# Early up-projection products in other PSUM banks, activation splits in another pool, kept norm chunks through DRAM: a two-layer encoder trunk on one Trainium2 core

## The chip, the cores and the metric

One core of one Trainium2 chip runs the whole program. The metric is device microseconds of one execution; 2956.74 us is the median of three runs of the kernel before (2948.64 to 2969.05).

The engines are TensorE (PE, matmuls into PSUM banks), VectorE (DVE), ScalarE (ACT), GpSimd (POOL), and SyncE (SP), which issues the DMAs. Each engine takes its instructions in a fixed order and waits at the head of it.

## What is computed

A trunk of two layers on x of 1024 tokens by 1024 features, all in fp32. Each layer mixes tokens by four head groups (pooling, chunked band attention, sparse attention, latent attention), projects them back, and then has a gated feed-forward part:

```python
    x = x + gt1 * (mix @ w_out[l])
    h = rmsnorm(x, g_ffn[l]) * (1.0 + sc2) + sh2
    f = (jax.nn.silu(h @ ffn_w1[l]) * (h @ ffn_w3[l])) @ ffn_w2[l]
    x = x + gt2 * f
return rmsnorm(x, g_final)
```

The feed-forward width is 2816, which is 22 blocks of 128 (NF = 22). `sc2`, `sh2` and `gt2` come from `c_act @ w_mod`, one vector for all tokens.

## The kernel before

**Numbers.** An fp32 product is made of three matmuls of a faster type: each operand is split in a high part, cast by ACT (L154 for weights to `wh`, L1102 to `ws`), and a low part, the difference, by POOL or DVE (L162, `wl`). A matmul below is one of 128x128 weights with 512 tokens. The activations stand transposed: features on partitions, tokens along the row, in two halves of 512 tokens.

**Up projection.** Pairs of blocks for both token halves are made by Strassen's scheme with seven products instead of eight (`product`, L1136), from sums of weights (`su`, `ws`) and sums of the normalised activations. `combos` (L1106) makes the activation sums u1 to u4 on DVE, from a chunk tile t0 of the first half and one t1 of the second. Some products need only the first token half: `up_pre` (L1167) makes those early, directly from w1 and w3 of a block, with its matmuls on L1181: 24 matmuls for one of the two weights, and their halves are copied to `xx`.

**Norm and what stands around it.** `norm2(g, r)` normalises token half g before the feed-forward part. It begins with the statistics: squares (ACT L359, DVE L360), their sum over features by matmuls with ones (L329), a reciprocal root on DVE, a broadcast by four L346 matmuls (two instructions each in the trace's count), and ACT's copy of it to R (L348). Then for k = 0 to 3 two chunks are made (L388, L394, L396, L399, L403) to a tile `t` of 512 KB and to the split `h`. For the first half `t` is kept to serve as t0 later. Between `norm2(0)` and `norm2(1)` stand the output projection of the second half (`proj_c(1)`, matmuls L184 to L186, the addition to x on DVE, L1090) and the early products. `norm2(1)` calls `combos` for each k.

**Down pass.** For each token half the 22 blocks f are summed over eight PSUM banks (L1331): `load(f)` gets a row of `ffn_w2` (DMA to `raw`, `wh` by ACT, `wl` by POOL), `act(f, g)` gets the activation from DRAM (`su`, then a split `ws`). x comes back from DRAM first (L1335). In the second half the first four f are kept (LATE = 4) until the eighth bank is free. Between the halves of layer 0 the statistics and the first norm of layer 1 run.

**Memory and order.** `slabs` is a pool of 34 tiles of 4 KB per partition, which x, h, t, `wh` and `wl` of the down pass share. A second pool in this part of the program has a ring of nine tiles `w` (`wslab`), two `su`, and there are two `raw` buffers. PSUM has eight banks under four names: mm 2, s 2, tr 3, pv 1. The output projection uses mm. The Tile scheduler simulates a timeline and so decides the order in each engine's queue; priorities (`high_priority`) and free buffers steer it. One queue, SP's, issues nearly all DMAs, in order: weights, spills, and the loads of `w_mod` whose sums (L271 to L274) are made for layer 1 during layer 0's feed-forward part.

`bank(i)` gives the bank of a product by its number:

```python
tag, bufs = (("mm", 2), ("s", 2), ("tr", 3), ("tr", 3), ("mm", 2), ("s", 2), ("tr", 3), ("pv", 1))[i]
```

Of the kernel before, what the change touches and what calls it, by code (L numbers as in the profile page):

```python
# [8 lines left out]
F32 = mybir.dt.float32  # L9
F32R = mybir.dt.float32r  # L10
# [8 lines left out]
DEPTH = 2  # L19
# [32 lines left out]
LATE = 4  # L52
LAST = 2
ALL7 = (1, 6, 5, 7, 2, 3, 4)
PRE = 2
# [14 lines left out]
class Trunk:  # L70
# [144 lines left out]
    def late_consts(self):  # L215
# [18 lines left out]
        if DEPTH > 1:  # L234
            self.xspill = self.dram.tile([KD, 128, S], F32, name="xspill")
        self.x2spill = [self.dram.tile([KD, 128, S], F32, name=f"x2spill{l}") for l in range(DEPTH)]
        self.aspill = [self.dram.tile([NF, 128, S], F32, name=f"aspill{l}") for l in range(DEPTH)]
        self.pspill = [self.dram.tile([2, 128, S], F32, name=f"pspill{l}") for l in range(DEPTH)]
# [859 lines left out]

    def split_tile(self, src, eng):

        w = self.wslab("ws")
        self.nc.scalar.activation(w[:, 0:512], src, AF.Copy)  # L1102
        self.sub_lo(w[:, 512:1024], src, w[:, 0:512], eng)
        return w

    def combos(self, t0, t1, b, db, c, out):  # L1106
# [3 lines left out]
        nc = self.nc  # L1110
# [12 lines left out]
        v.scalar_tensor_tensor(out=u2, in0=t1[:, 1, :], scalar=be, in1=u1, op0=ALU.add, op1=ALU.subtract)  # L1123
        split(2, u2, nc.vector)
        v.scalar_tensor_tensor(out=u3, in0=t1[:, 1, :], scalar=db[:, c:c + 1], in1=t1[:, 0, :],
                               op0=ALU.add, op1=ALU.subtract)
        split(3, u3, nc.gpsimd)
        v.scalar_tensor_tensor(out=u4, in0=t0[:, 1, :], scalar=be, in1=u2, op0=ALU.add, op1=ALU.subtract)
        split(4, u4, nc.vector)

# [37 lines left out]
    def up_pre(self, l, fa, H):  # L1168


        nc = self.nc
        xx = self.slab("xx", F32, (128, 2, 512))
        V = self.slab("v", F32, (128, 512))
        for i, name in enumerate(("w1", "w3")):
            wh, wl = self.load_w(self.a[name][l, fa])
            p = self.bank(i)
            for o, B in ((0, H[0][0:4]), (512, H[0][4:8])):
# [104 lines left out]
    def ffn(self, l, x, H, T, side, between):  # L1282
# [34 lines left out]
        def act(f, g):  # L1317
            t = self.rp.tile([128, 1024], F32, tag="su", bufs=NSUM, name=self.nm("su"))[:, 0:512]
            nc.sync.dma_start(out=t, in_=self.aspill[l][f][:, HALVES[g]])
            with self.tc.high_priority(offset=PRIO):  # L1320
                return self.split_tile(t, nc.vector)

# [52 lines left out]
    def mixer(self, l, x, H, spill, side, between, feed=None, first=None):  # L1375
# [193 lines left out]

        kept = []  # L1570
        HT = {}

        def norm2(g, r):
# [7 lines left out]
            for k in range(4):  # L1581
# [4 lines left out]
                if g == 0:  # L1586
                    kept.append(t)
                else:
                    self.combos(kept[k], t, b, db, k, HT)
                    kept[k] = None  # L1590
            for d in range(KD):
# [274 lines left out]
```

## Time and profile before

| | us |
|---|---|
| median of three runs (lowest, highest) | 2956.74 (2948.64, 2969.05) |
| profiled execution | 2957.3 |
| its span, from the first to the last instruction | 2955.4 |
| granted TensorE clock in it, mean | 0.935 |
| PE busy in the span | 2697.8 (91%) |
| VectorE, ScalarE, GpSimd busy | 1857.7, 1316.2, 1146.3 |
| moved by DMA | 305.92 MB |

Times in the trace count from the start of the span. Layer 0's first norm2 lies at 740 to 776 us, its up projection runs to 1268, its down pass to about 1554; layer 1's norm2 begins near 2188. A granted clock of 1.00 is 2.4 GHz, of 0.50 it is 1.2 GHz, and a value between is a mean over both. A bracket behind an instruction gives the engine's idle time just before it and what ended it. An engine that is idle off the critical path costs nothing.

### The profile page before, as it was taken

The numbers are of one execution on the slowest core, as the hardware profiler recorded it, in microseconds if no ns is written. First come the engines' busy times: TensorE is split into PE (matmuls) and PEld (weight loads), VectorE is DVE, ScalarE is ACT, GpSimd is POOL, SyncE is SP. The second block draws the span as 40 slices with busy tenths as digits, with TensorE's granted clock in tenths as the row PEclk, the third lists the DMA queues.
The fourth block names the chain that finished last, engine by engine and source line by source line (L and its number), as shares of the span: only waits on it lengthen the run. The fifth ranks groups of instructions, "written<-read, shape, count | busy, mean of one in ns | idle before, by whom it ended". The sixth has DMA issues, their size and how long they took to land.

```text
span 2955.4 us, 35110 instructions
## 1 busy us (share of the span) xinstructions
PE 2697.8 (91%) x12304; PEld 2144.3 (73%) x12304; DVE 1857.7 (63%) x3610; ACT 1316.2 (45%) x2536; POOL 1146.3 (39%) x672
## 2 busy tenths in 40 slices
PE   4897988899779999998899889998977999999998
PEld 3776757778547888887688667787765788888876
DVE  7579867775687566543335898788476743334452
ACT  4454767854423333332324547776443333333330
POOL 4242134441445555452623320113234655555630
PEclk9898979999769999999899989799988999999998
DMA  6102133233232344462431021112222222226540
GB/s 244 53 19 86 60 127 96 76 129 104 100 125 93 124 158 166 166 217 82 144 138 53 11 92 54 56 40 65 101 79 79 97 82 86 86 75 227 175 149 29
DMA packets 109873, 305.92 MB, mean 104 GB/s; under 512 B 13312, under 2 KB 14208, under 8 KB 109696
## 3 DMA queue, kind: packets, MB, share of 16 engines
q1 hardware_dynamic: 109696, 303.68, 30.1%
q8 instruction: 96, 1.57, 0.2%
q14 instruction: 81, 0.66, 0.1%
HBM read 245.11 MB, written 51.18 MB: 100 GB/s over the span
## 4 chain that ended last, share of the span: by engine, by line
PE 53%; DVE 10%; ACT 2%; DMA 2%; issue 2%; POOL 1%; SPq 0%; DVEq 0%; ACTq 0%; POOLq 0%
PE tr L1136 11%; PE mm L1136 7%; PE tr L1331 5%; PE s L1136 4%; PE pv L1136 3%; PE s L1331 3%; PE mm L1331 3%; DVE jv L544 2%; DMA raw<-ffn_w 2%; PE pv L1331 2%; PE mm L184 2%; PE mm L186 2%; PE mm L185 1%; PE tr L679 1%; DVE t L394 1%
## 5 line engine op out<-in xcount | busy, mean ns | idle before, releaser
L162 POOL TENSOR_TENSOR wl<-raw,wh 128x1024 fp32r<-128x1024 f32 (+1 forms) x158 | 375.6, 2381 | 629.0 <-ACT wh L154 349.6
L1136 PE MATMUL tr<-h,ws 128*128 128x512 f32 x1512 | 385.3, 403 | 20.3 <-POOL h L162 8.1
L1136 PEld LDWEIGHTS tr<-h,ws 128*128 128x128 f32 x1512 | 286.1, 190 | 105.0 <-POOL h L162 13.5
L162 POOL TENSOR_TENSOR ws<-su,ws 128x512 fp32r<-128x512 f32 x176 | 262.8, 1499 | 244.3 <-ACT ws L1102 220.7
L1102 ACT ACTIVATE ws<-su 128x512 fp32r<-128x512 f32 x264 | 163.3, 627 | 374.8 <-PE tr L1136 72.7
L162 DVE TENSOR_TENSOR ws<-su,ws 128x512 fp32r<-128x512 f32 x88 | 150.3, 1716 | 264.9 <-ACT ws L1102 264.7
L154 ACT ACTIVATE wh<-raw 128x1024 fp32r<-128x1024 f32 (+1 forms) x138 | 141.3, 1027 | 278.8 <-DMA raw<-ffn_w 182.9
L1136 PE MATMUL mm<-h,ws 128*128 128x512 f32 x912 | 237.6, 404 | 14.1 <-ACT ws L1102 8.9
L1136 PEld LDWEIGHTS mm<-h,ws 128*128 128x128 f32 x912 | 173.6, 192 | 61.7 <-ACT ws L1102 13.6
L162 POOL TENSOR_TENSOR ws<-raw,ws 128x512 fp32r<-128x512 f32 x108 | 157.1, 1458 | 127.9 <-ACT ws L1102 112.3
L541 ACT ACTIVATE ja<-score,tk_t 128x384 bf16<-128x384 f32 (+2 forms) x160 | 146.0, 913 | 121.8 <-DVE tk_t L563 86.1
L655 ACT ACTIVATE P<-P,mx 128x128 f32<-128x128 f32 (+1 forms) x192 | 142.9, 745 | 76.1 <-DVE mx L652 60.6
L1331 PE MATMUL tr<-ws,wh 128*128 128x512 f32 x528 | 167.6, 399 | 0.0
L682 ACT ACTIVATE Th<-tr 128x512 fp32r<-128x512 f32 (+3 forms) x288 | 127.8, 467 | 83.1 <-PE tr L679 75.2
L162 DVE TENSOR_TENSOR Tl<-tr,Th 128x512 fp32r<-128x512 f32 (+2 forms) x232 | 131.7, 587 | 32.3 <-ACT Th L682 31.4
L679 PE MATMUL tr<-ident,P 128*128 128x128 f32 x816 | 142.2, 290 | 7.1 <-DVE y L712 5.8
L1136 PE MATMUL s<-h,ws 128*128 128x512 f32 x528 | 141.9, 412 | 2.8 <-DVE yy L1224 2.8
L1102 ACT ACTIVATE ws<-raw 128x512 fp32r<-128x512 f32 x108 | 68.0, 629 | 169.7 <-PE tr L1136 105.7
L1331 PE MATMUL mm<-ws,wh 128*128 128x512 f32 x352 | 112.3, 399 | 14.0 <-ACT wh L154 14.0
L679 PEld LDWEIGHTS tr<-ident,P 128*128 128x128 f32 x816 | 107.2, 153 | 24.4 <-DVE y L712 7.4
L1136 PEld LDWEIGHTS s<-h,ws 128*128 128x128 f32 x528 | 103.0, 197 | 29.0 <-DVE yy L1224 3.2
L544 DVE TENSOR_SCALAR_CACHE_REDUCE jv<-up,tk_t 128x896 bf16<-128x896 bf16 (+3 forms) x128 | 120.8, 944 | 4.5 <-POOL up L522 1.9
(415 smaller groups left out, 6889.9 us busy)
## 6 DMA issues: line engine op xcount, KB each, us to landing
raw<-w SPq DMA_DIRECT2D x100, 512.0 KB, 3.5
raw<-ffn_w SPq DMA_DIRECT2D x88, 512.0 KB, 3.5
mraw<-w_mod SPq DMA_DIRECT2D x48, 512.0 KB, 6.0
t<-w_mod SPq DMA_DIRECT2D x96, 256.0 KB, 4.6
su<-aspill SPq DMA_DIRECT2D x88, 256.0 KB, 3.0
aspill<-act SPq DMA_DIRECT2D x32, 512.0 KB, 3.3
raw<-w_fm SPq DMA_DIRECT2D x30, 512.0 KB, 3.9
x2spill<-x SPq DMA_DIRECT2D x32, 256.0 KB, 2.2
```

The source lines that it names most:

```text
L154: self.nc.scalar.activation(out, in_, AF.Copy)
L162: (eng or self.nc.vector).tensor_tensor(out=out, in0=in_, in1=hi.bitcast(F32), op=ALU.subtract)
L184: self.nc.tensor.matmul(out, lh, rh, start=(i == 0), stop=False)
L186: self.nc.tensor.matmul(out, ll, rh, start=False, stop=(stop and i == n - 1))
L541: nc.scalar.activation(ja, score[t], AF.Sign, bias=c, scale=-1.0, accum_out=o)
L544: v.tensor_scalar(out=jv, in0=up[t] if step < 16 else score[t], scalar1=c, scalar2=0.0, op0=ALU.is_ge, op1=ALU.subtract, accum_out=o)
L655: nc.scalar.activation(P[:, 0:nk], P[:, 0:nk], AF.Exp, bias=m[:, j:j + 1], scale=-1.0, accum_out=st["rs"][:, i:i + 1])
L679: nc.tensor.transpose(p[:, i * 128:(i + 1) * 128], P[:, (kts[n] - k0) * 128:(kts[n] - k0 + 1) * 128], self.ident)
L682: nc.scalar.activation(Th[:, cs].bitcast(F32) if len(js) <= few else Th[:, cs], p[:, cs], AF.Copy)
L1102: self.nc.scalar.activation(w[:, 0:512], src, AF.Copy)
L1136: self.nc.tensor.matmul(p, u, r, start=first and k == 0 and i == 0, stop=k == 3 and i == 2, skip_group_check=not first)
L1331: nc.tensor.matmul(p, u, r, start=(f == 0 and i == 0), stop=(f == NF - 1 and i == 2))
```

## The change

There are three edits that move work; a fourth gives a name, `LOENG`, to the engine of two splits and leaves it as it is (`nc.vector`).

- A: `up_pre` takes bank 1 and 2 for the products of w1 and w3 (names s and tr) instead of 0 and 1 (mm and s).
- B: in the down pass `act` asks `split_tile` for a tile of `slabs` for the activation's split `ws` instead of one of the nine of the ring `w`.
- C: the four chunk tiles `t` of `norm2(0)` are stored to DRAM (`tspill`, 512 KB each) and loaded again as `t0` in `norm2(1)`, instead of being kept in four slabs between. Per layer these are four stores and four loads more.

```diff
+LOENG = lambda nc: nc.vector
...
+        self.tspill = [self.dram.tile([4, 128, 2, 512], F32, name=f"tspill{l}") for l in range(DEPTH)]
...
-    def split_tile(self, src, eng):
-
-        w = self.wslab("ws")
+    def split_tile(self, src, eng, base=False):
+
+        w = self.slab("ws", F32R) if base else self.wslab("ws")
         self.nc.scalar.activation(w[:, 0:512], src, AF.Copy)
         self.sub_lo(w[:, 512:1024], src, w[:, 0:512], eng)
         return w
...
-        split(2, u2, nc.vector)
+        split(2, u2, LOENG(nc))
...
-        split(4, u4, nc.vector)
+        split(4, u4, LOENG(nc))
...
         for i, name in enumerate(("w1", "w3")):
             wh, wl = self.load_w(self.a[name][l, fa])
-            p = self.bank(i)
+            p = self.bank(1 + i)
...
-                return self.split_tile(t, nc.vector)
+                return self.split_tile(t, nc.vector, True)
...
-        kept = []
         HT = {}
...
                 if g == 0:
-                    kept.append(t)
+                    nc.sync.dma_start(out=self.tspill[l][k], in_=t)
                 else:
-                    self.combos(kept[k], t, b, db, k, HT)
-                    kept[k] = None
+                    t0 = self.slab("t0", F32, (128, 2, 512))
+                    nc.sync.dma_start(out=t0, in_=self.tspill[l][k])
+                    self.combos(t0, t, b, db, k, HT)
```

The new lines move every line number behind them by one or two: L1181 is L1183 in the changed kernel, L329 is L331, L346 is L348, L154 is L155, L396 is L398, L1102 is L1104. The order of instructions changes at many places. Three of them follow, from layer 0.

PE before, at the statistics of `norm2(1)`: `pv` is the sum of squares, `mm_7532` the broadcast, `mm_7673` an early product of w1.

```order
L329 MATMUL pv_7506<-ones,t_7483 128x1 x4
L346 MATMUL mm_7532<-t_7533,ones 128x128
L1181 MATMUL mm_7673<-h_7093,wh_7669 128x512 x2
L1181 MATMUL mm_7673<-h_7093,wl_7670 128x512
L1181 MATMUL mm_7673<-h_7104,wh_7669 128x512 x2
L1181 MATMUL mm_7673<-h_7104,wl_7670 128x512
L1181 MATMUL mm_7673<-h_7115,wh_7669 128x512 x2
L1181 MATMUL mm_7673<-h_7115,wl_7670 128x512
L1181 MATMUL mm_7673<-h_7126,wh_7669 128x512 x2
L1181 MATMUL mm_7673<-h_7126,wl_7670 128x512
L346 MATMUL mm_7532<-t_7536,ones 128x128
L346 MATMUL mm_7532<-t_7539,ones 128x128
```

PE after, the same place (`tr_7720` is an early product of w3, `mm_7481` a piece of the output projection):

```order
L187 MATMUL mm_7481<-mh_7271,wl_6648 128x512
L1183 MATMUL tr_7720<-h_7107,wh_7716 128x512
L1183 MATMUL tr_7720<-h_7107,wl_7717 128x512
L1183 MATMUL tr_7720<-h_7119,wh_7716 128x512 x2
L1183 MATMUL tr_7720<-h_7119,wl_7717 128x512
L1183 MATMUL tr_7720<-h_7131,wh_7716 128x512 x2
L1183 MATMUL tr_7720<-h_7131,wl_7717 128x512
L331 MATMUL pv_7512<-ones,t_7489 128x1 x4
L348 MATMUL mm_7538<-t_7539,ones 128x128
L348 MATMUL mm_7538<-t_7542,ones 128x128
L348 MATMUL mm_7538<-t_7545,ones 128x128
L348 MATMUL mm_7538<-t_7548,ones 128x128
```

No early matmul stands between the four broadcast matmuls any more. Eight early matmuls stand behind the last piece of the output projection and directly ahead of L331, where there were none (in layer 1 there are 21). Further ahead, between the end of `norm2(0)`'s statistics and the first L763 (L765), there were 20 early matmuls, all into s; now there are 40, 20 into s and 20 into tr (in layer 1, 20 and 32).

SP's queue before, where `norm2(1)` has begun: the last store of x (L1592) and all loads of `w_mod` ahead of the next weight load `raw_7759<-w`, w3 of a block.

```order
L1592 DMA x2spill_252<-x_6593 128x512
L271 DMA t_7982<-w_mod 128x512
L271 DMA t_7983<-w_mod 128x512
L271 DMA t_7989<-w_mod 128x512
L271 DMA t_7990<-w_mod 128x512
L271 DMA t_7996<-w_mod 128x512
L271 DMA t_7997<-w_mod 128x512
L271 DMA t_8204<-w_mod 128x512
L271 DMA t_8205<-w_mod 128x512
L271 DMA t_8211<-w_mod 128x512
L1150 DMA raw_7759<-w 128x1024
```

SP's queue after, from the same store of x on:

```order
L1594 DMA x2spill_252<-x_6595 128x512
L1591 DMA t_2137_7561<-tspill_254 128x1024
L1591 DMA t_2149_7591<-tspill_254 128x1024
L1591 DMA t_2160_7619<-tspill_254 128x1024
L1591 DMA t_2172_7649<-tspill_254 128x1024
L273 DMA t_7996<-w_mod 128x512
L273 DMA t_7997<-w_mod 128x512
L273 DMA t_8003<-w_mod 128x512
L273 DMA t_8004<-w_mod 128x512
L273 DMA t_8010<-w_mod 128x512
```

The four loads of the chunk tiles (L1591) come between the store of x and the loads of `w_mod`. Of these nine stood ahead of w3's load, and now it is eleven: behind the last row shown six more, and then w3. The stores to `tspill` (L1588) stand earlier on the same queue, among the weight loads of the early products.

ACT before, at the seam between the halves of layer 0's down pass: the last chunk h of layer 1's norm, then the weights `wh` and activation splits `ws` of the second half. Three `ws` of that half stand further ahead, among the squares of the statistics.

```order
L396 ACTIVATE h_11723<-t_11724,modc_87 128x512
L154 ACTIVATE wh_11746<-raw_11744 128x1024
L154 ACTIVATE wh_11778<-raw_11776 128x1024
L154 ACTIVATE wh_11810<-raw_11808 128x1024
L154 ACTIVATE wh_11842<-raw_11840 128x1024
L154 ACTIVATE wh_11887<-raw_11885 128x1024
L154 ACTIVATE wh_11922<-raw_11920 128x1024
L1102 ACTIVATE ws_11848<-su_11846 128x512
L1102 ACTIVATE ws_11893<-su_11891 128x512
L154 ACTIVATE wh_11957<-raw_11955 128x1024
```

ACT after, the same place:

```order
L398 ACTIVATE h_11737<-t_11738,modc_87 128x512
L155 ACTIVATE wh_11760<-raw_11758 128x1024
L1104 ACTIVATE ws_11766<-su_11764 128x512
L155 ACTIVATE wh_11792<-raw_11790 128x1024
L1104 ACTIVATE ws_11798<-su_11796 128x512
L155 ACTIVATE wh_11824<-raw_11822 128x1024
L1104 ACTIVATE ws_11830<-su_11828 128x512
```

The casts of weights and activations alternate now, and none of the second half's `ws` stands ahead of the h any more.

## Rows read from the trace of the kernel before

**Rows 1.** The page, part 1: busy us, share of the span, instructions.

```profile
PE 2697.8 (91%) x12304; PEld 2144.3 (73%) x12304; DVE 1857.7 (63%) x3610; ACT 1316.2 (45%) x2536; POOL 1146.3 (39%) x672
```

**Rows 2.** Stretches: length, busy PE, PEld, DVE, ACT, POOL; clock, DMA share, GB/s.

```profile
747.00:776.00 29.00, 13.80 (x33) 8.80 (x34) 25.54 (x30) 11.43 (x21) 20.49 (x12) 0.52 0.22 73
...
778.73:810.00 31.27, 31.05 (x132) 24.23 (x131) 12.77 (x18) 11.75 (x19) 11.56 (x7) 1.00 0.37 121
...
862.00:902.00 40.00, 25.98 (x88) 19.26 (x89) 37.50 (x58) 9.96 (x18) 22.08 (x14) 0.79 0.53 177
...
962.00:1332.00 370.00, 370.00 (x1586) 297.66 (x1585) 211.25 (x332) 120.89 (x187) 198.40 (x122) 1.00 0.48 167
...
1421.00:1554.00 133.00, 133.00 (x601) 108.25 (x600) 45.98 (x50) 39.00 (x49) 51.37 (x21) 1.00 0.44 153
...
2368.00:2812.00 444.00, 444.00 (x1903) 357.11 (x1902) 185.82 (x215) 147.52 (x222) 237.86 (x140) 1.00 0.36 122
```

**Rows 3.** PE groups of layer 0's h chain: busy, mean ns, idle before, releasers.

```profile
L1181 PE MATMUL s<-h,wh 128*128 128x512 f32 x14 | 9.0, 688 | 10.9 <-DVE h L403 4.2 <-ACT h L396 2.9 <-POOL h L162 2.6
```

**Rows 4.** Timeline, layer 0 statistics: start, length, engine, line; [idle before <-releaser].

```profile
812.39 1.46 PE L329 MATMUL pv<-ones,t 128*128 128x1 f32 x8 [2.29 <-DVE t L360]
...
816.92 1.20 PE L1181 MATMUL mm<-h,wh 128*128 128x512 f32 x2
...
821.06 0.83 PE L346 MATMUL mm<-t,ones 128*128 128x128 f32 x6
...
821.92 0.60 ACT L348 ACTIVATE t<-mm 128x512 f32<-128x512 f32 x1 [10.31 <-PE mm L346]
...
822.55 0.75 DVE L394 SCALAR_TENSOR_TENSOR t<-x,acol,t 128x512 f32<-128x512 f32 x1 [5.55 <-ACT t L348]
```

**Rows 5.** Timeline of DVE, combos of layer 0: two chunk starts.

```profile
837.48 1.76 DVE L394 SCALAR_TENSOR_TENSOR t<-x,acol,t 128x512 f32<-128x512 f32 x1
...
845.31 1.76 DVE L394 SCALAR_TENSOR_TENSOR t<-x,acol,t 128x512 f32<-128x512 f32 x1
```

**Rows 6.** Timeline of PE, the same place in layer 1.

```profile
2250.07 1.20 PE L1181 MATMUL mm<-h,wh 128*128 128x512 f32 x2
...
2254.41 0.83 PE L346 MATMUL mm<-t,ones 128*128 128x128 f32 x6
...
2297.64 1.22 PE L1136 MATMUL mm<-h,ws 128*128 128x512 f32 x2 [3.37 <-DVE su L1164]
```

**Rows 7.** Timeline of PE and ACT, seam of layer 0's down pass.

```profile
1414.77 1.22 PE L1331 MATMUL mm<-ws,wh 128*128 128x512 f32 x2 [14.04 <-ACT wh L154]
...
1413.05 0.72 ACT L396 ACTIVATE h<-t,modc 128x512 fp32r<-128x512 f32 x1 [0.95 <-DVE t L394]
```

**Rows 8.** Timeline of PE, start of the down pass: 12 matmuls apart.

```profile
1267.90 0.62 PE L1331 MATMUL mm<-ws,wh 128*128 128x512 f32 x2
...
1270.70 0.63 PE L1331 MATMUL mm<-ws,wh 128*128 128x512 f32 x2
```

**Rows 9.** Timeline of SP's queue and PE, behind the combos of layer 0.

```profile
806.28 4.96 SPq L1592 DMA_DIRECT2D x2spill<-x  x5
...
848.49 10.16 SPq L271 DMA_DIRECT2D t<-w_mod  x9
...
869.84 1.22 PE L1136 MATMUL mm<-h,ws 128*128 128x512 f32 x2 [8.92 <-ACT ws L1102]
```

**Rows 10.** The page, part 6: KB each, median us to landing.

```profile
aspill<-act SPq DMA_DIRECT2D x32, 512.0 KB, 3.3
```

**Rows 11.** Groups and DMA issues, layer 0's second down half.

```profile
L154 ACT ACTIVATE wh<-raw 128x1024 fp32r<-128x1024 f32 x22 | 23.3, 1061 | 55.2 <-DMA raw<-ffn_w 47.7 <-PE pv L1331 7.5
...
L1102 ACT ACTIVATE ws<-su 128x512 fp32r<-128x512 f32 x19 | 11.8, 622 | 27.2 <-PE pv L1331 25.4 <-DMA su<-aspill 1.7
...
L162 POOL TENSOR_TENSOR wl<-raw,wh 128x1024 fp32r<-128x1024 f32 x21 | 51.4, 2448 | 71.6 <-DVE x L1354 41.0 <-ACT wh L154 30.5
...
raw<-ffn_w SPq DMA_DIRECT2D x18, 512.0 KB, 3.4
```

## Prediction

> **What bounds the kernel now.** I read the page's busy shares first, then busy time by stage, then TensorE's (PE's) idle times in the stages where it isn't full, and then who released it there.
>
> PE is busy 91% of the 2955.4 us span, the next engine 63% [rows 1]. That share is an average over two kinds of stage. The reader is to see in the table of stretches that the up projections (962 to 1332, and 2368 to 2812 with layer 1's down pass) have PE busy for all of their 370 and 444 us, at granted clock 1.00. Layer 0's second down half from 1421 on is the same: 133 of 133 us [rows 2]. Nothing off PE can make these shorter; it can only make them longer, by starving PE. What can be won lies in three places where PE waits:
>
> 1. The *h chain*: `norm2(0)` makes the normalised chunks h of the first token half on ACT, DVE and POOL while PE has the early products (L1181) as its only work. In layer 0 PE is busy 13.80 of 29.00 us there at clock 0.52, DVE 25.54 [rows 2]. The 20 early matmuls in it have 10.9 us of idle time ahead of them [rows 3].
> 2. The *statistics of norm2(1) and the combos*. PE waits 2.29 us for the last square (L329) [rows 4]. A while later one L346 matmul is issued, then **12 early products (816.92 to 821.06, 4.14 us)**, and only then the other three L346 matmuls, whose sum ACT copies at 821.92 to R [rows 4]. DVE, which makes everything from R on, stands idle 5.55 us [rows 4]. From there DVE sets the pace: one chunk k begins 8 us after the other (837.48, 845.31) [rows 5]. Layer 1 has the same picture, 2250.07 to 2254.41 [rows 6].
> 3. The *seam* between the halves of layer 0's down pass: PE idle 14.04 us until ACT has cast the first weight (wh), which stands in ACT's order behind the last h chunk (1413.05) [rows 7].
>
> **The change part by part.**
>
> *A, banks.* The early products go from banks mm and s to s and tr. PSUM has the same pieces; what changes is where the scheduler can put the second product of each pair. The output projection's pieces use mm, so in the old banks two of the four products stood behind them. After, products in s and tr alternate inside the h chain: 40 matmuls in layer 0 instead of 20, and 32 instead of 20 in layer 1. And the 12 products that parted L346 stand ahead of L329, and some early products stand behind the last projection piece, 8 in layer 0 (the first of the order excerpts) and 21 in layer 1. Three prices, for layer 0:
>
> - *The 12 moved matmuls*: out of the R chain goes what they took there, 4.14 us. Ahead of L329 they cost 2.80 us, since 12 back-to-back matmuls take 2.80 us, 0.233 each, at full clock (1267.90 to 1270.70) [rows 8], and the stretch ahead of L329 is at 1.00 [rows 2].
> - *Cover*: the 2.29 us ahead of L329 are the time in which the last projection piece is added and squared [rows 4]. In the new order 8 matmuls (1.9 us) stand in it, so of the 2.80 us 0.9 are left: with nothing else changed L329 would start at 813.3 instead of 812.39.
> - *Absorption*: 20 more matmuls go into the h chain. At half clock, twice 0.233 us each, they need 9.3 us; 10.9 us of idle time lies there [rows 3]. Whether each fits depends on which gap it meets, so the bounds are none and all; I take half. Ten matmuls are 10 x 0.233 = 2.3 us less work behind the chain (0 to 4.7).
>
> So PE reaches L329 1.4 us earlier (0.9 later, 2.3 earlier; bounds 0.9 later and 3.8 earlier). From L329 to R took 821.92 - 812.39 = 9.5 us and takes 9.5 - 4.1 = 5.4. R, and with it every DVE step of the combos, comes **5.5 us earlier** (3.2 to 7.9). In layer 1, with the idle time ahead of L329 as in layer 0 and wholly covered (0.5 of the 2.80 us left): 12 more in the chain, half of them absorbed, 1.4 us; L329 earlier by 1.4 - 0.5 = 0.9; R chain shorter by 4.34 [rows 6]; **5.2 us** (3.8 to 6.6).
>
> Does that reach the end? In layer 1 the combos' last matmuls and 24 early products are followed by one idle time of 3.37 us that DVE's own chain ends, and from then on PE is full, as [rows 2] has it from 2368 on [rows 6]. Everything there hangs on DVE's combos, so it passes on. In layer 0 it doesn't all pass: PE waits 8.92 us for splits of raw<-w3, and that load stands on SP's queue behind nine w_mod loads that take 10.16 us to issue (1.13 each) [rows 9].
>
> *C, the spill.* Four chunk tiles of 512 KB go out behind the h chain and come back ahead of the combos: 16 transfers over both layers, 8 MB. No row shows such a load; the nearest is aspill's store of 512 KB, 3.3 us from issue to landing [rows 10]. The loads are issued behind the last x2spill, which is out by 806.28 + 4.96 = 811.2 [rows 9]. The first is wanted at the combos' first DVE step behind R, 822.55 [rows 4], or 817.0 with R 5.5 us earlier. 811.2 + 3.3 = 814.5: hidden, by 2.5 us; the bounds are nothing and, at twice that landing time, 0.8 us. Without this cover it would cost what it is late. The third waits for a buffer that chunk 0 frees (behind 822.55), the fourth for one that chunk 1 frees (before 837.48); they land 3.3 us behind that, and chunks 2 and 3 begin 8 us apart [rows 5], so they are hidden by 4 us and more. The stores fall where the DMA engines have a share of 0.22 [rows 2] and take no engine's time. What C does cost: SP issues four more rows ahead of w_mod, and eleven instead of nine w_mod rows ahead of raw<-w3 (second excerpt). Two rows at 1.13 us are 2.3 us [rows 9]. w_mod's buffers come free with the combos, so its start moves with R. **Layer 0 keeps 5.5 - 2.3 = 3.2 us** (0 to 7.9).
>
> *B, the activation splits in slabs.* SP's queue now strictly alternates activation and weight. Per activation row f PE needs 24 matmuls, 5.6 us. Supply of a weight: 3.4 us from issue to landing, ACT 1.06, POOL 2.45, through two raw buffers: 6.9 / 2 = 3.5 us [rows 11]. The activation is half as wide and its split on ACT takes 0.62 [rows 11]. Slabs: in layer 0's second half eight hold x and eight the h of the next norm, two the projection's weights; 16 of 34 remain, three per row, 5.3 rows ahead. There the first four rows are kept for the eighth bank (LATE), so at the narrowest point 1.3 rows are ahead: row 4, and nothing whole of row 5. Row 5's casts need 1.06 + 2.45 = 3.5 us from the first freed slab; PE has 9 matmuls of the kept rows and row 4 meanwhile, 2.1 + 5.6 = 7.7 us. Hidden, by 4.2 us. At the seam, the first row's activation split goes behind the h chain too: before, ACT had made three ahead of it; after, it casts wh, ws, wh, ws behind it (third excerpt). So PE restarts one ws, **0.6 us**, later (bounds: 0, and 0.6 + 2.45 for a low part that is waited for). The 14.04 us themselves stay, since wh is still behind the last h [rows 7].
>
> The scheduler also reorders layer 1's attention, with no matmul added; I price it at 0, with bounds of one idle time as in [rows 6], 3.4 us either way.
>
> **Sum**, on the profiled execution (2957.3 us; 2955.4 span and 1.9 around it): -3.2 - 5.2 + 0.6 = -7.8, so 2949.5. The median of the runs shown, 2956.74, is 0.56 us under its 2957.3: **2949 us**.
>
> **The rivals.**
>
> - *Nothing net.* In layer 0 DVE is busy 37.5 of the 40 us behind the combos (862 to 902) with w_mod's sums and the splits [rows 2]. If its total work sets the end, an earlier R is eaten there; and if the h chain absorbs nothing, layer 1 keeps 3.8. Then it is -3.8 + 0.6 at most: 2953.5 to 2957. For: DVE's share. Against: layer 1 has no w_mod there.
> - *The change doesn't do what it says*: slabs freed by C are used by no one, and the down pass was full anyway. Then B and C are worth 0 and A alone makes the sum above; the time is the same, 2948 to 2950.
> - *Slower: the narrow point of B.* If the two raw loads don't overlap, since su and raw wait in one queue for each other's buffers, a row costs 6.9 us of supply against PE's 5.6: 1.3 us for 17 rows is 22 us in layer 0's second half, 2971; the layer-1 halves have more slabs. In all four halves 88 us, 3037. It decides where supply passes 5.6 us a row. Against: 3.5 us.
> - *Slower: the clock.* The groups of s and tr that alternate with short waits between could hold the clock at 1.2 GHz past the h chain, through the dense stretch behind it, where PE is busy 31.05 of 31.27 us at 1.00 [rows 2]. At half clock this is 31 us more in each layer: 2949 + 62 = 3011. Against it: the h chain runs at half clock already (0.52), with one bank in turn, and the clock rose in the dense stretch, which follows in either order. The Trainium skill (TensorE: Matmul & The Clock Gate, section "A second HAM failure mode: psum-queue depth-cycling") tells of such a kernel: matmul groups went through the banks in turn, PE was idle for a little between them, and the clock swung between its two levels. No run here shows a swing in a stretch without idle time; by that page the 3011 would be due, by the rows of this trace the 2949.
> - *Faster.* A denser h chain lifts the clock before the dense stretch, and the seam's 14.04 us shrink because two weight splits find slabs ahead of the h's. Worth at most half of PE's 13.80 busy us in each layer's chain and half of the seam: 6.9 + 6.9 + 7, so 2928; over 1% needs the combos' DVE pace changed too, which the order doesn't show.
>
> **How the numbers follow.** Forecast as summed: 0.50; its own range is 2942 (-7.9 - 6.6 without the seam) to 2953, where the next case begins. That holds the case that the change doesn't do what it says, 0.10. Nothing net (to 2960): 0.20. Faster than 2942: 0.14, of it 0.09 by over 1%. Slower than 2960: 0.16, of it B's narrow point 0.08, the clock 0.03, layer 1's attention 0.05; by over 1% 0.08. The three runs shown lie 20 us apart, so 1% (29.6 us) is about what a measurement of this kernel can tell from no change. Range: 2930 to 2968, which leaves out about 0.1 on either side. Faster by over 1% 0.09, within 1% 0.83, slower by over 1% 0.08.
>
> **What would show it.** L329 and L346 together without L1181 between, R some 5 to 6 us sooner behind the h chain's start; PE's idle time ahead of raw<-w3's splits in layer 0 at 11 us (8.92 + 2.3, by the w_mod rows); layer 1's full stretch beginning 5 to 6 us sooner after the h chain begins; the seam's idle time near 14.6 us; PE full in all four down halves. Wrong if idle time shows inside a down half, if t0 loads release DVE's L1121, or if the h chain grows because PE falls behind it.

## The result, and the profile after

The changed kernel takes 2918.82 us, the median of four runs (2913.12 to 2920.89), beside 2953.65 us for the kernel before. The ratio is 0.987, with a 95% interval from 0.983 to 0.9911. That is 34.8 us faster. The forecast of 2949 us, with its range from 2930 to 2968, missed it on the fast side.

The profiled execution took 2920.89 us with a span of 2919.1. PE's row of the page's first part, to be held against [rows 1] (busy time, share of the span, instructions of each engine):

```profile
PE 2675.5 (92%) x12290; PEld 2139.9 (73%) x12304; DVE 1892.8 (65%) x3610; ACT 1313.8 (45%) x2536; POOL 1142.5 (39%) x672
```

PE's busy time fell by 22.3 us, from 2697.8, and the program has the same matmuls (that the row counts 12290 instead of 12304 is records missing from the trace; the weight loads, PEld, are 12304 in both). So more than half of the gain isn't a wait that went away. Three rows of stretches in the kernel after show where (length, then busy time and count of PE, PEld, DVE, ACT and POOL; granted clock, DMA share, GB/s): the up projection, then the down pass of layer 0 and of layer 1.

```profile
1000.00:1100.00 100.00, 100.00 (x430) 80.51 (x429) 62.17 (x110) 32.28 (x54) 54.40 (x37) 1.00 0.39 138
...
1270.00:1370.00 100.00, 100.00 (x443) 82.89 (x442) 39.46 (x19) 29.74 (x38) 48.18 (x20) 1.00 0.45 156
...
2660.00:2901.00 241.00, 241.00 (x1073) 199.86 (x1072) 106.61 (x95) 72.62 (x95) 97.70 (x41) 1.00 0.42 144
```

The same two stretches of layer 0 in the kernel before:

```profile
1000.00:1100.00 100.00, 100.00 (x430) 80.43 (x429) 67.48 (x123) 31.05 (x52) 53.64 (x36) 1.00 0.45 162
...
1280.00:1380.00 100.00, 100.00 (x429) 80.38 (x428) 27.15 (x13) 27.57 (x32) 48.59 (x21) 1.00 0.42 145
```

Look at the count in brackets, not at the busy share. All four rows of 100 us say PE busy 100 of 100 us at granted clock 1.00. Yet the down pass issues 443 matmuls where it issued 429. One matmul of 0.39 us reaches in from before the stretch, so the distance from start to start is 100.39 / x: **234.0 ns before, 226.6 ns after in the down pass, 233.5 ns in both in the up projection**. The down pass has 22 blocks x 24 matmuls x 2 halves x 2 layers = 2112 matmuls, and 2112 x 7.4 ns = 15.6 us.

The page's groups say the same. This is the largest group of the down pass, before and then after (busy time, mean ns of one; idle time before them):

```profile
L1331 PE MATMUL tr<-ws,wh 128*128 128x512 f32 x528 | 167.6, 399 | 0.0
```

```profile
L1333 PE MATMUL tr<-ws,wh 128*128 128x512 f32 x528 | 164.1, 392 | 0.0
```

The whole difference of the profiled pair, by places in PE's order (from the starts of the same instructions in both traces):

| place | forecast, us | measured, us |
|---|---|---|
| up to the last broadcast matmul group of `norm2(0)`, layer 0 | 0 | -3.2 |
| from there until PE is full, layer 0 | -3.2 | -7.3 |
| down pass, layer 0, first and second half | 0 | -4.0, -3.8 |
| seam of layer 0 | +0.6 | -0.4 |
| attention of layer 1 | 0 | -1.4 |
| layer 1, until PE is full | -5.2 | -5.4 |
| up projection, layer 1 | 0 | 0 |
| down pass of layer 1, pace | 0 | -8.1 |
| down pass of layer 1, seam | 0 | -2.0 |
| tail | 0 | -0.6 |
| sum | -7.8 | -36.2 |

The span fell by 36.3 us. The three edits change nothing ahead of the first row's place; its 3.2 us are a difference between two executions, and the runs of one kernel here lie 8 to 24 us apart. Where PE was forecast to win, at the two lead-ins, it won 12.7 us instead of 8.4. Where the forecast had 0 it won 15.9 us by pace and 2.0 at layer 1's seam.

Now the lead-in of layer 0, which answers to [rows 4]. Timeline of the statistics of `norm2(1)` after (start, length, engine, line; idle before and what ended it):

```profile
804.91 1.87 PE L331 MATMUL pv<-ones,t 128*128 128x1 f32 x8 [2.00 <-DVE t L362]
...
809.40 2.08 PE L348 MATMUL mm<-t,ones 128*128 128x128 f32 x8 [2.62 <-DVE t L346]
...
811.51 0.60 ACT L350 ACTIVATE t<-mm 128x512 f32<-128x512 f32 x1 [7.38 <-PE mm L348]
812.14 0.75 DVE L396 SCALAR_TENSOR_TENSOR t<-x,acol,t 128x512 f32<-128x512 f32 x1 [2.21 <-ACT t L350]
```

L331 and L348 stand together with no early product between, and ACT's copy to R comes 811.51 - 804.91 = 6.6 us behind L331, where it took 9.5. The first chunk on DVE (L396) is released by R and by no DMA.

SP's queue and PE behind the combos, which answer to [rows 9]; then PE where it becomes full in layer 1 [rows 6] and at the seam of layer 0 [rows 7]:

```profile
803.85 23.34 SPq L1591 DMA_DIRECT2D t<-tspill  x4
...
838.60 11.43 SPq L273 DMA_DIRECT2D t<-w_mod  x11
...
850.08 0.91 SPq L1152 DMA_DIRECT2D raw<-w  x2
```

```profile
861.11 1.22 PE L1138 MATMUL mm<-h,ws 128*128 128x512 f32 x2 [9.39 <-ACT ws L1104]
```

```profile
2272.01 0.72 PE L1138 MATMUL mm<-h,ws 128*128 128x512 f32 x2 [3.31 <-ACT ws L1104]
```

```profile
1399.83 0.79 PE L1333 MATMUL mm<-ws,wh 128*128 128x512 f32 x1 [14.56 <-ACT ws L1104]
```

### The profile page after: what moved, and what is told of

Its sections match the earlier page's. It is cut to its first block, busy times and chain, and to the rows that moved or that the text cites. A ratio compares the mean times of both kernels' runs of the same rounds, so it can differ in the third digit from the quotient of the medians.

```text
span 2919.1 us, 35152 instructions
## 1 busy us (share of the span) xinstructions
PE 2675.5 (92%) x12290; PEld 2139.9 (73%) x12304; DVE 1892.8 (65%) x3610; ACT 1313.8 (45%) x2536; POOL 1142.5 (39%) x672
## 5 line engine op out<-in xcount | busy, mean ns | idle before, releaser
L1104 ACT ACTIVATE ws<-su 128x512 fp32r<-128x512 f32 x264 | 163.6, 626 | 347.7 <-PE tr L1138 70.4
L163 DVE TENSOR_TENSOR ws<-su,ws 128x512 fp32r<-128x512 f32 x88 | 183.9, 2091 | 174.9 <-ACT ws L1104 174.6
L155 ACT ACTIVATE wh<-raw 128x1024 fp32r<-128x1024 f32 (+1 forms) x138 | 141.5, 1026 | 252.4 <-DMA raw<-ffn_w 165.2
L1138 PE MATMUL mm<-h,ws 128*128 128x512 f32 x912 | 239.2, 407 | 13.1 <-ACT ws L1104 12.7
L1104 ACT ACTIVATE ws<-raw 128x512 fp32r<-128x512 f32 x108 | 67.9, 629 | 169.0 <-PE tr L1138 106.1
L1333 PE MATMUL mm<-ws,wh 128*128 128x512 f32 x352 | 110.0, 392 | 14.6 <-ACT ws L1104 14.6
```

The lines of the kernel that those rows point to most:

```text
L155: self.nc.scalar.activation(out, in_, AF.Copy)
L163: (eng or self.nc.vector).tensor_tensor(out=out, in0=in_, in1=hi.bitcast(F32), op=ALU.subtract)
L1138: self.nc.tensor.matmul(p, u, r, start=first and k == 0 and i == 0, stop=k == 3 and i == 2, skip_group_check=not first)
L1333: nc.tensor.matmul(p, u, r, start=(f == 0 and i == 0), stop=(f == NF - 1 and i == 2))
```

## The experiments

First theory for the pace: an address. Edit B moves the activation's split `ws` from the ring `w` into `slabs`, where `wh` and `wl` lie, so that both operands of a down matmul come from one pool. In the built program the slabs begin at byte 1152 of each partition and the pool of the ring at byte 180512. Rival: the pace follows from supply, since the ring's nine tiles no longer hold activations and weights both. The second question is what A, B and C are each worth.

### One edit at a time

**B alone.** In the kernel before, `act` takes its tile from `slabs`:

```diff
-    def split_tile(self, src, eng):
+    def split_tile(self, src, eng, base=False):
...
-        w = self.wslab("ws")
+        w = self.slab("ws", F32R) if base else self.wslab("ws")
...
-                return self.split_tile(t, nc.vector)
+                return self.split_tile(t, nc.vector, True)
```

> The kernel before with edit B alone (activation splits of the down pass in slabs). If the faster matmuls of the down pass come from B, whichever way: 0.2266 us a matmul in all four down halves, 16 us, and 2 us at the seam of layer 1, less 0.6 at the seam of layer 0: about 2954 - 17 = 2937. The lead-ins (740 to 900 and 2180 to 2300) as before. If the rate is a by-product of A or C: 2954.

Measured: 2937.66 us, ratio 0.9934 (0.9909 to 0.9959), 20.0 us faster. The down pass shows the new pace:

```profile
1275.00:1375.00 100.00, 100.00 (x443) 82.84 (x442) 38.30 (x17) 31.34 (x38) 50.33 (x21) 1.00 0.48 164
```

The halves of layer 0 took 119.49 and 121.14 us and layer 1's down pass 241.05 (before 123.46, 126.11 and 251.15), 19.0 us together. So B carries the whole gain of the down pass, and it needs neither A nor C.

**A and C without B.**

```diff
...
-                return self.split_tile(t, nc.vector, True)
+                return self.split_tile(t, nc.vector)
```

> The changed kernel without edit B (splits in the ring again). If the parts add up: the lead-ins gain 8 us in layer 0 and 5 us in layer 1, the down pass stays at 0.234 us a matmul: 2954 - 13 = 2941. If B is what mattered and A with C gain only what was forecast: 2946.

Measured: 2945.18 us, ratio 0.997 (0.9952 to 0.9988). The down pass is at the old pace, 429 matmuls in 100 us (1270 to 1370), and takes the old time, 123.47 and 126.09 us in layer 0 and 249.68 in layer 1. The pace goes with B.

**A alone.** The only edit is the bank number:

```diff
-            p = self.bank(i)
+            p = self.bank(1 + i)
```

> The kernel before with edit A alone (early products in banks s and tr). The forecast put the whole gain of the lead-ins down to A: then 2941 to 2946, as with A and C. Rival: A needs C's slabs to put w3's products into the h chain; then the h chain holds fewer than 40 early matmuls and this run lies nearer to 2954.

Measured: 2943.17 us, ratio 0.995 (0.9927 to 0.9973), 14.5 us faster. Counted from `norm2(0)`, the combos start 6.7 us sooner in layer 0 and 6.5 us sooner in layer 1 (7.2 and 6.3 in the changed kernel). The down pass is untouched (123.46 us for its first half). A makes the lead-ins' gain by itself.

**C alone.**

```diff
...
-                    kept.append(t)
+                    nc.sync.dma_start(out=self.tspill[l][k], in_=t)
...
-                    self.combos(kept[k], t, b, db, k, HT)
-                    kept[k] = None
+                    t0 = self.slab("t0", F32, (128, 2, 512))
+                    nc.sync.dma_start(out=t0, in_=self.tspill[l][k])
+                    self.combos(t0, t, b, db, k, HT)
```

> The kernel before with edit C alone (chunk tiles through DRAM). The forecast: C gives nothing by itself and costs two w_mod rows ahead of raw<-w3 in layer 0, 2.3 us, so 2957 to 2960. Rival: the freed slabs let the scheduler move early products ahead by themselves, and the lead-in of layer 0 becomes shorter by some us: 2950.

Measured: 2960.83 us, ratio 1.0011 (0.9991 to 1.0031). C costs and wins nothing that ten runs can tell.

**A and B without C** (edit C undone in the changed kernel).

> The changed kernel without edit C (the chunk tiles kept in slabs again). A alone was 14 us faster than the kernel before, B alone 20, C alone no different. If the parts add up and C is idle: 2958 - 34 = 2924, within a few us of the changed kernel's 2919. If A or B use the slabs that C frees: clearly slower than that, 2935.

Measured: 2923.68 us, ratio 0.988 (0.9859 to 0.9902), against 0.987 with C. The slabs that C frees are worth nothing that can be told. The parts add up: 14.5 for A and 20.0 for B are 34.5, and the change gave 34.8.

### The address by itself

These kernels move no instruction: a small unused tile shifts the pool of the ring and the `su` (and the pools of the first projections and of the attention, which begin at the same address in their turn), and every engine's order stays the same but for one DVE memset for each such tile. `slabs`, `raw` and the chunk temporaries keep their addresses. In the kernel before, with N = 8, 16, 24 or 56 floats (32, 64, 96, 224 bytes):

```diff
+        self.gap = ctx.enter_context(tc.tile_pool(name="gap", bufs=1)).tile([128, N], F32, tag="gap", name=self.nm("gap"))
+        tc.nc.vector.memset(self.gap, 0.0)
         self.reg = None
```

**32 bytes.**

> The kernel before, with one unused tile of 32 bytes per partition ahead of the pool that holds the weight and split tiles; it moves that pool from address 180512 to 180544, a multiple of 64, and changes no instruction's place in any engine's order (one memset more on DVE). Theory 1 (address): the down pass of the changed kernel runs at 0.2266 us a matmul instead of 0.2343 because its moving operand ws no longer begins at 32 modulo 64. Then this kernel has the same rate in the down pass, and the up projection, whose weights ws lie in that pool too, goes from 0.2333 to about 0.2266 as well: 2112 x 7.7 ns + 3360 x 6.7 ns = 16 + 22 us, and some 4 us in other projections, so 2954 - 42 = 2912. Theory 2 (pool or traffic: the down pass is faster since ws lies in the same pool as the weights, or since other engines write elsewhere): nothing changes, 2954, and both rates stay at 0.233 to 0.234.

Measured: 2937.56 us, ratio 0.9936 (0.9913 to 0.9958). Up projection, then down pass:

```profile
1000.00:1100.00 100.00, 100.00 (x437) 81.83 (x436) 67.53 (x122) 31.67 (x53) 55.10 (x37) 1.00 0.43 152
...
1275.00:1375.00 100.00, 100.00 (x430) 80.55 (x430) 26.56 (x13) 27.98 (x33) 51.05 (x21) 1.00 0.44 152
```

The expected 226.7 ns in the down pass did not come: it went to 233.5. But the up projection went from 233.5 to 229.7 ns. So an address that nothing but a gap moved does set the pace of a full PE, and "aligned to 64 bytes" is the wrong rule for it.

**96 bytes**, in the kernel before and in the changed one.

> The kernel before with an unused tile of 96 bytes ahead of the pool of splits, so that the pool begins at 180608, a multiple of 128 (with 32 bytes more it began at 64 modulo 128; the rates were then 0.2333 us a matmul in the down pass and 0.2300 in the up projection). No instruction changes its place. Theory 1b (address modulo 128): with all operands at multiples of 128 the down pass runs at 0.2267 us a matmul, as in the changed kernel, and the up projection too: 2112 x 7.6 ns + 3360 x 6.6 ns + some 4 us in other projections = 42 us, 2957 - 42 = 2915. Theory 2 (the two pools lie apart, and it is the distance or the pool that counts): 0.233 to 0.234 in both, 2957 to 2937.

> The changed kernel with the same 96 bytes. Theory 1b: its down pass is at 0.2267 already and stays; the up projection goes from 0.2333 to 0.2267, 3360 x 6.6 ns = 22 us, and other projections some 4 us: 2919 - 26 = 2893. Theory 2: 2919.

Measured: the kernel before with the gap takes 2913.79 us, ratio 0.9862 (0.9826 to 0.9897); the changed kernel with the gap 2886.94 us, ratio 0.9772 (0.9741 to 0.9802), **the fastest of all, ahead of both kernels**. Their up projections and down passes:

```profile
1000.00:1100.00 100.00, 100.00 (x442) 82.58 (x441) 63.24 (x112) 31.07 (x52) 55.90 (x39) 1.00 0.46 158
...
1255.00:1355.00 100.00, 100.00 (x443) 82.84 (x442) 28.82 (x15) 29.19 (x35) 51.17 (x22) 1.00 0.46 158
```

```profile
1000.00:1100.00 100.00, 100.00 (x442) 82.67 (x441) 68.23 (x127) 29.53 (x49) 54.12 (x36) 1.00 0.52 187
...
1250.00:1350.00 100.00, 100.00 (x443) 82.86 (x442) 40.53 (x19) 29.32 (x36) 48.23 (x20) 1.00 0.46 156
```

Without B, without any change of supply, the down pass runs at 226.6 ns. That settles address against supply. One gap of 96 bytes alone wins 44.4 us, more than the whole change. By the pace alone, the 3408 products of the up projections x 6.4 ns would give 21.8 us and the 2112 of the down pass 15.6. But of the 15.6 the trace shows only 8.8: layer 0's halves take 119.45 and 121.93 us (123.46 and 126.11 before), layer 1's down pass with its seam 250.55 (251.15). There PE now has 4.7 us of idle time at the seam and runs at half clock behind it. Layer 1's down pass of this kernel and the half-clock stretch in it, then the longest of the six waits:

```profile
2643.02:2893.60 250.58, 245.89 (x1073) 201.73 (x1071) 109.11 (x92) 71.86 (x94) 101.58 (x42) 0.99 0.39 135
2777.40:2784.30 6.90, 6.60 (x20) 5.54 (x21) 2.94 (x17) 0.00 (x0) 0.00 (x0) 0.51 0.32 116
```

```profile
2777.70 1.86 PE L331 MATMUL pv<-ones,t 128*128 128x1 f32 x8 [2.58 <-DVE t L362]
```

The rest of the 44.4 lies elsewhere, part of it perhaps in the 1296 matmuls of the first projections, whose weights moved by the same 96 bytes; no run divides it further.

**64 bytes.**

> The kernel before with 64 bytes: the pool begins at 180576, 96 modulo 128, and again at 32 modulo 64. If the address modulo 64 or 128 sets the rate and not the added tile: as before, 0.234 us a matmul in the down pass and 0.233 in the up projection. If the tile itself helps: like the kernel with 32 bytes, 0.230 in the up projection.

Measured: 2952.5 us in one run; 431 matmuls in 100 us in either stretch, 232.9 ns. No gain.

**224 bytes.** By now the likely rule was that the two pools' begins must agree, modulo 128 or modulo 256; this gap tells them apart.

> The kernel before with 224 bytes ahead of the pool of splits: the difference to the pool of h is 128 modulo 256 (with 96 bytes it was 0 modulo 256). If the period of the effect is 128 bytes: 0.2267 us a matmul in the up projection and the down pass, 2914 as with 96 bytes. If it is 256: a rate above that, 0.230 to 0.234, 2940 or more.

```profile
1000.00:1100.00 100.00, 100.00 (x431) 80.42 (x430) 66.15 (x120) 31.68 (x53) 52.82 (x37) 1.00 0.42 146
...
1275.00:1375.00 100.00, 100.00 (x430) 80.48 (x429) 27.54 (x13) 28.09 (x33) 50.28 (x21) 1.00 0.43 149
```

Measured: 2953.97 us in one run, 232.9 and 233.5 ns. The period is 256, not 128.

**Absolute address or difference?** Two gaps in the changed kernel: 32 bytes ahead of `slabs` and 96 more behind it, so that both pools move and their difference becomes a multiple of 256; and the first gap alone, so that both move by 32 bytes and the difference stays.

```diff
+        self.g1 = ctx.enter_context(tc.tile_pool(name="gapa", bufs=1)).tile([128, 8], F32, tag="gapa", name=self.nm("gapa"))
+        tc.nc.vector.memset(self.g1, 0.0)
         self.slabs = ctx.enter_context(
...
+        self.g2 = ctx.enter_context(tc.tile_pool(name="gapb", bufs=1)).tile([128, 24], F32, tag="gapb", name=self.nm("gapb"))
+        tc.nc.vector.memset(self.g2, 0.0)
         self.raws = ctx.enter_context(
```

> The changed kernel with the pool slabs moved by 32 bytes (and 96 bytes behind it, so that the pools behind it keep their address modulo 128). No instruction changes its place, and the activation split ws and the weights of the down pass still lie in one pool. Address theory: the down pass falls back from 0.2267 us a matmul to 0.233 or more, 2112 x 7 ns = 15 us or more, so 2934 or more; the up projection, with both operands off, stays at 0.233 or gets slower. Pool theory (one pool is what makes it fast): it stays at 0.2267, 2919.

> The changed kernel with every pool moved by the same 32 bytes: the pool of h now begins at 32 modulo 128 and that of the splits at 64, and their difference stays 32 modulo 128 in size. No instruction changes its place. Difference theory: nothing changes, the up projection stays at 0.2333 us a matmul and the down pass at 0.2267, 2919. Absolute theory (some start addresses are good, such as 32 and 32): the up projection changes its rate.

Measured, one run each: 2887.73 and 2922.74 us. The first fits neither theory as it was put: the down pass kept the fast pace, as the pool theory said, but the up projection took it too, which neither had expected. Up projection of the first, then of the second:

```profile
1000.00:1100.00 100.00, 99.83 (x441) 82.31 (x439) 68.19 (x118) 29.51 (x49) 56.09 (x37) 1.00 0.50 179
```

```profile
1000.00:1100.00 100.00, 100.00 (x430) 80.44 (x429) 64.54 (x117) 31.71 (x53) 53.14 (x36) 1.00 0.39 140
```

It is the difference. Both pools stand at other addresses than in the 96-byte kernel, and the pace is the fast one; moved together, they leave the pace at the slow one. All of it in one table (D is the begin of the ring's pool less that of the slabs, modulo 256; ns from start to start):

| kernel | D | up | down |
|---|---|---|---|
| before | 160 | 233.5 | 234.0 |
| + 32 bytes | 192 | 229.7 | 233.5 |
| + 64 bytes | 224 | 232.9 | 232.9 |
| + 96 bytes | 0 | 227.1 | 226.6 |
| + 224 bytes | 128 | 232.9 | 233.5 |
| changed (down: one pool, difference 0) | 160 | 233.5 | 226.6 |
| changed, + 96 bytes | 0 | 227.1 | 226.6 |
| changed, both gaps | 0 | 227.3 (99.83 us busy) | 227.1 (x442) |
| changed, both pools + 32 | 160 | 233.5 | 226.6 (x443) |

One count more or less is 0.5 ns, so the figures between 232.9 and 234.0 hardly differ. The mean over all pairs of neighbours in a whole trace (2000 and more each, without those over 260 ns) is finer: 226.7 to 226.8 where the difference is 0, 230.0 in the up projection at D = 192, 232.9 to 234.3 at all others. In the up projection h, from the slabs, streams past weights in the ring, and in the down pass `ws`, from the ring, past weights in the slabs. So the address of the streaming operand less that of the weights is 256 - D in the first and D in the second, and the table holds all eight multiples of 32: 0 is fast, 64 (D = 192, up) a little faster than the rest, and 192 (D = 192, down) is like the others.

### What B and C are worth once the address is right

Both have 96 bytes: the first is the changed kernel without B, the second without C.

> The changed kernel without B, with the pool of splits 96 bytes further, so that all matmul operands begin at multiples of 128. If B's gain is only the address of the operand ws, this run equals the changed kernel with the 96 bytes, 2887. Rival: B also lets the second half's splits be cast ahead of the seams; then this run is slower by the idle times at the seam of layer 1 (some 2 us in the kernel before, with a stretch at half clock behind it), less 0.6 at layer 0's: 2889 to 2897.

> A and B with the 96 bytes, without C. If C is idle: the same as all three with the 96 bytes, 2887. If C helps (its slabs) or hurts (its transfers, two w_mod loads ahead of w3) this run tells by how much: 2880 to 2895.

Measured: 2901.2 us, ratio 0.9801 (0.9778 to 0.9823), and 2895.63 us, ratio 0.9795 (0.9767 to 0.9822), against 0.9772 (0.9741 to 0.9802) with all three. Without B the pace is the fast one throughout, yet the median is 14.3 us longer, above the rival's 2889 to 2897. The two intervals overlap, so the times alone don't tell it from none. The traces show the place: layer 1's down pass with its seam takes 250.84 us without B and 241.01 with it. PE waits there (timeline of PE at the seam of layer 1, without B):

```profile
2768.53 0.73 PE L1334 MATMUL s<-ws,wh 128*128 128x512 f32 x2 [2.66 <-DVE x L1357]
...
2781.78 1.05 PE L332 MATMUL pv<-ones,t 128*128 128x1 f32 x8 [2.58 <-DVE t L363]
```

With all three, PE has no idle time there at all. In the kernel before, too, PE waited at this seam, though its clock stayed at 1.00 there and the half clock of the expectation is not in its trace:

```profile
2820.43 1.05 PE L329 MATMUL pv<-ones,t 128*128 128x1 f32 x8 [1.96 <-DVE t L360]
```

So B has a second effect. In all seven traces of kernels with B this pass takes 240.99 to 241.05 us. In all nine without it takes 249.68 to 256.75, and of these the two at the fast pace, 250.55 and 250.84, are about as long as the 251.15 of the kernel before: the seam takes back what the pace gives. PE waits there for DVE's additions to x and its squares; why B's order spares PE these waits, no run separates. C's 8.7 us can't be told from none, since the intervals overlap.

## Why the prediction was wrong

**The step that failed** is the sentence that nothing off PE can make the full stretches shorter, and with it the price of 0.233 us a matmul, taken from one pair of rows [rows 8] as the engine's own pace. From it followed "B hidden" and a down pass worth 0. The engine was full and its matmuls still took 3% longer than in the runs with difference 0. The clock was at its upper level (granted 1.00, 2.4 GHz) on both sides, so it isn't the clock. The missing term is 2112 x 7.4 ns = 15.6 us, and 15.9 us were measured. In layer 1 its half shows only because B also ends the waits at the seam; the gap of 96 bytes alone shortened that pass by 0.6 us. No rival named the term: all asked whether B could starve PE, none whether the place of an operand could change PE's pace. The Trainium skill would have led the same way: in TensorE: Matmul & The Clock Gate, section "Step-by-step: what each phase is for", PE has two independent read ports, one for the streaming operand and one for the weights, and a weight load takes nothing from the running matmul. Here the pace did hang on the addresses of the two operands relative to each other, 226.6 against 234.0 ns; whether the ports have to do with it, no run shows.

**A, layer 0: right mechanism, too small** (3.2 forecast, 7.3 measured, inside 0 to 7.9). Counted from `norm2(0)`'s broadcast (749.06 before, 745.86 after):

- *Absorption* was taken as half of 20 matmuls. All 20 were absorbed: the first L763 (L765) starts 26.2 us behind the broadcast, where it was 25.9, and PE's busy time in the chain rose from 13.80 of 29.00 us [rows 2] to the first row here. The clock rose to 1.00 within the chain, 21.5 us behind the broadcast instead of 29.7. The second row is the stretch behind it:

```profile
745.86:774.00 28.14, 20.29 (x61) 13.87 (x62) 24.08 (x29) 11.95 (x23) 18.50 (x11) 0.62 0.43 149
776.00:800.00 24.00, 24.00 (x105) 19.39 (x104) 14.15 (x17) 10.58 (x17) 10.23 (x6) 1.00 0.47 145
```

- *Cover* did not work as told. The eight matmuls stand behind the last projection piece, and L331 still waits 2.00 us (2.29 before), because the additions and squares of the last pieces end later: L331 starts 4.26 us behind the last projection matmul (804.91 - 800.65), where it was 2.68. All the same L331 came 4.3 us sooner than before (forecast 1.4); the 20 absorbed matmuls and the earlier clock both work that way, and no run parts them.
- *From L331 to R*: 6.6 us, forecast 5.4. The 4.14 us of early products are gone, but L331 and L348 took 1.87 and 2.08 us, where the row of before had 0.83 for six of the eight broadcasts [rows 4]. PE had been idle twice just ahead, and the granted clock was 0.70 over 800 to 812. R came 7.2 us sooner, forecast 5.5.
- *The w_mod rows*: eleven instead of nine, as forecast, 11.43 against 10.16 us: 1.3 lost, not 2.3. PE's wait there was 9.39 us; 11 had been forecast. PE restarts 5.5 us sooner (861.11, 869.84 before). The other 1.8 of the 7.3 lie between there and the full stretch, where one wait of 1.00 us is gone; the forecast had nothing there, and no run says what makes them.

**A, layer 1: the sum right, its parts not.** 5.4 us measured, 5.2 forecast; the last idle time is 3.31 us (3.37 before). But L331 came 3.3 us sooner (forecast 0.9), the way from it to R got 3.0 us shorter (forecast 4.3), and 0.9 of R's 6.3 us didn't reach the full stretch. The misses cancel, so that the sum fits is luck.

**The seam of layer 0: right at the restart.** 14.56 us against "near 14.6"; it hangs on the activation's split now, as forecast. The whole seam still got 0.4 us shorter, not 0.6 longer, since the wait ahead of its statistics (L329, now L331) fell from 3.25 to 2.29 us, which the forecast hadn't asked about. **Layer 1's seam** was left out of the sum: 1.96 us of idle time there are gone.

**C: right.** It is hidden. The first chunk on DVE behind R isn't released by a load, although SP's queue stood 23.34 us over the four loads, and C alone measured 1.0011.

**The rivals.** B's narrow point did not come: PE is busy 241 of 241 us in layer 1's down pass and has no idle time inside any half. Nor did the slow clock: the stretch behind the h chain, 776 to 800 us, is full at granted clock 1.00 (the second row above). Of the faster rival one half came, a denser chain (clock 0.62 against 0.52); the seam's 14.04 us did not shrink. What made the time fall below its 2928 was in no case at all.

**What stays open.** The runs show that the difference of the two operands' addresses sets the pace, with its period and its values at the multiples of 32. They don't show which part of the chip makes it so, nor why 64 is a little faster than the others, nor what B does at layer 1's seam.

## What to carry to other kernels

A stretch in which PE is busy 100% at full clock isn't at its floor until its matmuls per microsecond are compared with the best stretch of the same shape; 429 and 443 in 100 us look alike in the busy share. Where a buffer moves to another pool, ask what its address becomes relative to the other operand's: here a gap of 96 bytes, which made the difference a multiple of 256 bytes, was worth 44 us by itself and, by the medians of two series, 32 us on top of the change. When a change bundles a move of buffers with a change of order, run the move with the order held still, since the gain may be the address.

## What the runs showed of the hardware

A 128x128 weight with 512 fp32 columns took 226.6 to 227.3 ns from start to start where the two operands lay a multiple of 256 bytes apart within a partition, and 229.7 to 234.0 ns at the other seven multiples of 32 bytes (229.7 at 64 alone, streaming operand less weights). The common offset made no difference in the one run that changed it: moved by 32 bytes together, the operands kept their pace. The busy share, the granted clock (1.00) and the order of instructions were the same in both cases.
